# Layer 0's scales and shifts: modulation weights loaded into the array, conditioning vectors streamed

## The chip, the cores and the metric

The kernel runs on one core of one Trainium2 chip. The metric is device time in microseconds (us) of one execution: the median of several runs, lower is better. The engines of the core are TensorE (PE; its weight loads are shown apart as PEld), VectorE (DVE), ScalarE (ACT), GpSimd (POOL) and SyncE (SP, which issues nearly all DMAs here). They run their own instruction lists in program order and wait for each other by semaphores.

## What is computed

The reference is a two-layer diffusion backbone block over 1024 latent tokens and 256 context tokens, model width D = 1024, all in float32. Cut to what matters here, layer 0 begins with

```python
def adaln(cvec, w, b):                 # w: (1024, 3072)
    m = jax.nn.silu(cvec) @ w + b
    return jnp.split(m[..., None, :], 3, axis=-1)     # shift, scale, gate

def modulate(x, g, shift, scale):
    return rmsnorm(x, g) * (1.0 + scale) + shift

sh, sc, gt = adaln(c, ada_w_e[0], ada_b_e[0])         # for the latent tokens
h = modulate(x, norm_e[0], sh, sc)
shc, scc, gtc = adaln(c_ctx, ada_w_e[0], ada_b_e[0])  # for the context tokens
hc = modulate(ctx, norm_e[0], shc, scc)
# h and hc then go through h @ in_e (six column blocks), a pooling mixer, a gated conv mixer, out_e
```

The change concerns the shift and the scale: two vectors (silu(c) and silu(c_ctx), 1024 long) times a 1024 x 2048 matrix. Layer 1 and the gate of layer 0 get theirs elsewhere, on VectorE.

## The kernel before

Activations lie with the 1024 features on partitions (8 tiles of 128, index k) and the tokens along the free side, so shift and scale are wanted as columns: `mode[:, m, s]` holds feature 128*m+p on partition p for stream s (0 latent, 1 context).

The modulation matrix `ada_e` is read in 16 slabs of 128 x 1024 f32 (512 KB), `part` 1 (scale) first, then `part` 0 (shift), each k = 0..7. `ada(part, k)` (L452) takes one of three slots (`adp`, L433), issues the slab's DMA on SP's queue (L455), and issues two matmuls (L457): the loaded side is `cs[:, k, :]` (128 x 2: the two silu'd vectors), the streamed side is half of the slab (512 columns). The sums over k gather in four PSUM tiles `pr` of the pool `psd` as two rows of 512 columns. Each f32 matmul appears in the trace as two pairs of a weight load and a stream, so 32 matmuls are 64 pairs.

`ada_end(part)` (L459) turns the rows into columns. For each half q: the row is copied out of PSUM (L462, by the helper at L231 on ACT for q = 0, L233 on DVE for q = 1), four transposes on PE (L464) put 128 x 2 columns into `pm`, and DVE adds the bias into `mode` (L467). After part 1 two more DVE operations (L417) make `Ae` = norm * (1 + scale).

The order of the work is the program order of L504 to L532, the same on every queue:

- L504: slabs of part 1, and between them the loads of x's first 512 tokens (`fetch`, L447); the first projection weight is loaded (L294).
- L508: ACT squares x (L483) and DVE adds (L485); L509 `ada_end(1)`.
- L510: a ones matrix on PE (L312) sums the squares over partitions, then 1/rms on ACT and DVE (L375 to L387).
- L511: DVE scales x by `Ae` and 1/rms (L512). L513: slabs of part 0.
- L516 to L519: ACT casts projection weights to their high halves (`wh`, L267) and POOL makes the low halves (`wl`, L268); SP issues the loads of the next weight, of tokens 512 to 1023 and of the context.
- L520 `ada_end(0)`. L524: ACT adds the shift and rounds (`hi`, L526), DVE makes the remainder (`lo`, L527), k by k. In between the squares of the second token block run on ACT, POOL (L481) and DVE.
- From there the projections: `dense` (L302), for each k three fp32r products of 128 x 512 (`wl` by hi, `wh` by lo, `wh` by hi). After the first 36 of them PE is given the ones matmuls for the second token block and for the context (L312), then goes on.

The `dense` tiles of L302 come from the same PSUM pool as the four `pr` tiles.

Of the kernel before, what the change touches and what calls it, by code (L numbers as in the profile page):

```python
# [8 lines left out]
F32 = mybir.dt.float32  # L9
F32R = mybir.dt.float32r  # L10
AF = mybir.ActivationFunctionType
ALU = mybir.AluOpType
# [167 lines left out]
class Kern:  # L180
# [241 lines left out]
    def layer_even(self, es):  # L422
        tc, nc, A = self.tc, self.nc, self.A
        self.psd = es.enter_context(tc.tile_pool(name="psd", bufs=4, space=PSUM))
        psa = es.enter_context(tc.tile_pool(name="psa", bufs=2, space=PSUM))
        mode = self.cp.tile([128, 24, 2], F32, name="mode")
        cs = self.cp.tile([128, 8, 2], F32, name="cs")
        h = self.slots()
        ctx_norm = ExitStack()
        nrm = ctx_norm.enter_context(tc.tile_pool(name="nrm", bufs=2, side="right"))  # L430
        xin = ctx_norm.enter_context(tc.tile_pool(name="xin", bufs=2, side="right"))
        w0p = ctx_norm.enter_context(tc.tile_pool(name="w0p", bufs=1, side="right"))
        adp = ctx_norm.enter_context(tc.tile_pool(name="adp", bufs=3, side="right"))  # L433
        pm = psa.tile([128, 24, 2], F32, tag="pm", name="pm", bufs=1)
        nc.scalar.activation(out=cs[:, :, 0], in_=self.vcol("c", 0, 8), func=AF.Silu)
        nc.scalar.activation(out=cs[:, :, 1], in_=self.vcol("c_ctx", 0, 8), func=AF.Silu)

# [9 lines left out]
                nc.sync.dma_start(out=x, in_=(A["xT"] if src == "x" else A["ctxT"])[k, :, c0:c0 + n])  # L447
                xs.setdefault(b, []).append(x)

        pr = [self.psd.tile([128, 512], F32, tag="d", name="pr") for _ in range(4)]  # L450

        def ada(part, k):  # L452

            w = adp.tile([128, 1024], F32, tag="ad", name="ad")
            nc.sync.dma_start(out=w, in_=A["ada_e"][k, :, 1024 * part:1024 * part + 1024])  # L455
            for q in range(2):
                nc.tensor.matmul(pr[2 * part + q][0:2], lhsT=cs[:, k, :], rhs=w[:, 512 * q:512 * q + 512], start=(k == 0), stop=(k == 7))  # L457

        def ada_end(part):  # L459
            row = nrm.tile([2, 1024], F32, tag="row", name="row", bufs=1)  # L460
            for q in range(2):
                self.copy(("act", "dve")[q], row[:, 512 * q:512 * q + 512], pr[2 * part + q][0:2])  # L462
                for m in range(4 * q, 4 * q + 4):
                    nc.tensor.transpose(pm[:, 8 * part + m, :], row[:, 128 * m:128 * m + 128], self.cst("eye")[0:2, 0:2])  # L464
                o = slice(8 * part + 4 * q, 8 * part + 4 * q + 4)
                b = self.vcol("ada_b_e", 8 * part + 4 * q, 4).unsqueeze(2).to_broadcast([128, 4, 2])
                nc.vector.tensor_tensor(out=mode[:, o, :], in0=pm[:, o, :], in1=b, op=ALU.add)  # L467
            if part:
                self.Ae = self.mod_cols(mode, "norm_e", "Ae")

# [33 lines left out]
        for k in range(8):  # L504
            ada(1, k)
            fetch(XB[0], (k,))
        next(self.wit)
        *_, acc = squares(XB[0])  # L508
        ada_end(1)  # L509
        rs = rstd(XB[0], acc)  # L510
        for k, x in enumerate(X(XB[0])):  # L511
            nc.vector.scalar_tensor_tensor(out=x, in0=x, scalar=self.Ae[:, k, 0:1], in1=rs, op0=ALU.mult, op1=ALU.mult)  # L512
        for k in range(8):  # L513
            ada(0, k)
# [3 lines left out]
        next(self.wit)  # L518
        fetch(CB[0])  # L519
        ada_end(0)  # L520
        sq1 = squares(XB[1], (1, 3, 5))
        nc.vector.tensor_copy(mode[:, 16:24, 0], self.vcol("ada_b_e", 16, 8))
# [14 lines left out]
        def lines(t, off, pitch, src, c0, n, sh=0):  # L537

            if src == "x":
                p0 = off + pitch * (c0 // 64)  # L540
                a = t[:, p0 + sh:p0 + sh + 1]
                return bass.AP(tensor=a.tensor, offset=a.offset, ap=[list(a.ap[0]), [pitch, n // 64], [1, 64]])
            p0 = off + pitch * 16 + c0 + sh
            return t[:, p0:p0 + n]

        def flat(t, src, c0, n, as_lines=True):
            o = c0 + (0 if src == "x" else T)
            v = t[:, o:o + n]
            return v.rearrange("p (r t) -> p r t", t=64) if (src == "x" and as_lines) else v
# [18 lines left out]
        def first(b, side=True, order=(0, 1, 2)):  # L568

            ds = [self.dense(ws[i][0], rhs, (b,), ws[i][1]) for i in order]  # L570
            for _ in range(8 if side else 0):
                for d in ds[:2]:
                    for _ in range(3):
                        yield next(d)
            for d in ds:
                yield from d

        d = first(XB[0])
# [11 lines left out]
        d = first(XB[1])  # L590
# [5 lines left out]
        d = first(CB[0], False, (1, 0, 2))  # L596
# [55 lines left out]
        for i in range(4):  # L652
# [5 lines left out]
            bufs = [sa, sb]  # L658
            for lv in range(i + 1):
# [6 lines left out]
                m = 1 << lv  # L666
# [19 lines left out]
            w = next(self.wit)  # L686
            for _ in self.dense(w, rhs, BLK, lambda s, c0, n, ps: nc.vector.tensor_tensor(
                    out=lines(Q, 1, 65, s, c0, n), in0=ps.rearrange("p (r t) -> p r t", t=64) if s == "x" else ps,
                    in1=flat(gcs, s, c0, n), op=ALU.mult)):
                pass  # L690
            ada_on(2)
            for s, c0, n in (("x", 0, T), ("c", 0, TC)):
                o = flat(cv, s, c0, n)
                nc.vector.tensor_scalar(out=o, in0=lines(Q, 1, 65, s, c0, n), scalar1=self.vcol("sconv_w", 4 + i),
                                        scalar2=None, op0=ALU.mult)
                for tap, sh in ((0, -1), (2, 1)):
                    nc.vector.scalar_tensor_tensor(out=o, in0=lines(Q, 1, 65, s, c0, n, sh), scalar=self.vcol("sconv_w", 4 * tap + i),
                                                   in1=o, op0=ALU.mult, op1=ALU.add)
            w = next(self.wit)
            for _ in self.dense(w, rhs, BLK, lambda s, c0, n, ps: nc.vector.tensor_tensor(  # L700
                    out=flat(cv, s, c0, n, False), in0=ps, in1=flat(cv, s, c0, n, False), op=ALU.mult)):
                pass
            w = next(self.wit)
# [20 lines left out]
        for b in (BLK[0], BLK[2], BLK[1]):  # L724
# [3 lines left out]
            o = c0 + (0 if s == "x" else T)  # L728
# [70 lines left out]
        for m in range(4, 8):  # L799
# [6 lines left out]
            if m == 6:  # L806
                w = [next(self.wit)]
# [1591 lines left out]
```

## Time and profile before

| | us |
|---|---|
| median of 3 runs | 1560.08 |
| lowest, highest | 1555.54, 1568.76 |
| profiled execution, its own time | 1569.38 |
| its span (first to last instruction) | 1567.6 |
| mean granted TensorE clock in it | 0.938 of 2.4 GHz |

The rows below are from that one profiled execution. Times are from the start of the span. In a timeline a row is a run of like instructions, merged: start, length, engine, line, operation, tiles, shapes, count, and in brackets the engine's idle time just before and what ended it. The clock column gives the granted TensorE clock as a share of 2.4 GHz, 0.50 being 1.2 GHz; its records don't reach back to the first matmuls, where it shows 1.00 for want of one.

### The profile page before, as it was taken

Reading aid. Unit: us, or ns where it says so; the run is one execution under the profiler, and the core shown is the slowest. Engines: PE = TensorE matmul, PEld = TensorE weight load, DVE = VectorE, ACT = ScalarE, POOL = GpSimd, SP = SyncE. Lnnn points to the kernel's source line nnn. Section 1 sums busy time; section 2 is a strip of 40 time slices with the busy share of each in tenths; the row PEclk is TensorE's granted clock in tenths of the full one; section 3 lists DMA queues with packets and bytes.
Section 4 is the critical chain, followed back from the end, with each engine's and each line's share of the span. In section 5 each row is a group of like instructions: output and inputs, shape, how many; then the busy total and the mean of one; then the engine's idle time right before and its main releaser. Section 6 shows DMA issues by size and latency. Waiting matters only on the chain. (4 is left out here: it accounts for less than half of the span.)

```text
span 1567.6 us, 32131 instructions
## 1 busy us (share of the span) xinstructions
PE 1393.9 (89%) x12820; PEld 1092.7 (70%) x12820; DVE 1006.2 (64%) x1681; ACT 621.7 (40%) x1242; POOL 662.7 (42%) x925
## 2 busy tenths in 40 slices
PE   6899999999999998987988878898997988886996
PEld 1488888888888786865766656676775766674775
DVE  3746544347513732499999974878497677688567
ACT  2541111111423533445655521343454543557534
POOL 1352424252644532355565522755566246406004
PEclk9999999999999999999999989899998987878999
DMA  7413223222333112244544666655555566674233
GB/s 264 148 65 126 95 89 121 94 81 95 97 132 128 55 44 76 69 139 148 188 135 144 210 215 160 147 164 139 155 142 138 161 158 166 200 236 125 76 94 108
DMA packets 167894, 208.72 MB, mean 133 GB/s; under 512 B 38112, under 2 KB 129632, under 8 KB 167616
## 3 DMA queue, kind: packets, MB, share of 16 engines
q1 hardware_dynamic: 166448, 205.09, 43.4%
q8 instruction: 101, 1.65, 0.5%
q10 hardware_dynamic: 1296, 1.57, 0.3%
q14 instruction: 49, 0.40, 0.1%
HBM read 149.20 MB, written 55.44 MB: 131 GB/s over the span
## 5 line engine op out<-in xcount | busy, mean ns | idle before, releaser
L302 PE MATMUL d<-sx,wh 128*128 128x512 f32 x1152 | 361.6, 395 | 2.5 <-DVE sx L527 1.4
L302 PEld LDWEIGHTS d<-sx,wh 128*128 128x128 f32 x1152 | 217.2, 189 | 53.2 <-POOL sx L397 1.8
L302 PE MATMUL d<-sx,wl 128*128 128x512 f32 x576 | 229.8, 399 | 4.5 <-DVE u L822 2.7
L1396 POOL TENSOR_TENSOR tmp<-X,Bc 128x120 f32<-128x120 f32 (+2 forms) x300 | 122.1, 407 | 204.1 <-DMA Bc<-ED 181.9
L268 POOL TENSOR_TENSOR wl<-wr,wh 128x1024 fp32r<-128x1024 f32 x37 | 95.5, 2582 | 185.7 <-ACT wh L267 176.2
L992 PE MATMUL d<-sx,wh 128*128 128x512 f32 x512 | 167.5, 409 | 0.0
L1936 PE MATMUL d<-sx,wh 128*128 128x512 f32 x384 | 142.5, 439 | 0.0
L1397 POOL TENSOR_TENSOR X<-X,tmp 128x120 f32<-128x120 f32 (+2 forms) x300 | 120.1, 400 | 23.5
L302 PEld LDWEIGHTS d<-sx,wl 128*128 128x128 f32 x576 | 108.9, 189 | 29.7 <-issue 3.3
L628 DVE SCALAR_TENSOR_TENSOR junk<-wra,cb 128x1024 bf16<-128x1024 f32 x56 | 91.5, 1635 | 52.1 <-DMA wra<-in_ada_o 30.5
L992 PEld LDWEIGHTS d<-sx,wh 128*128 128x128 f32 x512 | 102.3, 200 | 23.9 <-issue 2.9
L992 PE MATMUL d<-sx,wl 128*128 128x512 f32 x256 | 116.2, 454 | 0.0
L302 PE MATMUL d<-sc,wh 128*128 128x256 f32 x576 | 104.1, 281 | 0.0
L1936 PE MATMUL d<-sx,wl 128*128 128x512 f32 x192 | 84.1, 438 | 7.4 <-DVE wl L1910 7.4
L1957 DVE SCALAR_TENSOR_TENSOR acc<-hc,vec,acc 128x960 f32<-128x960 f32 (+14 forms) x120 | 89.3, 769 | 1.1
L302 PEld LDWEIGHTS d<-sc,wh 128*128 128x128 f32 x576 | 88.8, 190 | 1.4
L1936 PEld LDWEIGHTS d<-sx,wh 128*128 128x128 f32 x384 | 75.6, 203 | 16.9 <-issue 0.2
L267 ACT CAST wh<-wr 128x1024 fp32r<-128x1024 f32 x37 | 38.7, 1045 | 117.3 <-PE d L302 86.8
L302 PE MATMUL d<-sc,wl 128*128 128x256 f32 x288 | 81.0, 281 | 0.0
L1498 PE MATMUL sc<-w,bk 64*128 64x128 f32 (+1 forms) x640 | 55.9, 313 | 21.7 <-DMA bk<-BKD 14.1
L1498 PEld LDWEIGHTS sc<-w,bk 64*128 64x128 f32 x640 | 47.0, 212 | 30.2 <-issue 24.9
L1512 DVE TENSOR_TENSOR w<-sc,cstb 64x256 f32<-64x256 f32 x80 | 33.8, 422 | 43.1 <-PE sc L1498 26.4
(380 smaller groups left out, 2909.8 us busy)
## 6 DMA issues: line engine op xcount, KB each, us to landing
wr<-in_in_o SPq DMA_DIRECT2D x32, 512.0 KB
wr<-in_in_e SPq DMA_DIRECT2D x24, 512.0 KB
wra<-in_ada_o SPq DMA_DIRECT2D x24, 512.0 KB
BKD<-bk SPq DMA_DIRECT2D x40, 256.0 KB
BTD<-X SPq DMA_DIRECT2D x20, 512.0 KB
bk<-BKD SPq DMA_DIRECT2D x40, 256.0 KB
Bc<-ED SPq DMA_DIRECT2D x20, 512.0 KB
bkt<-BTD SPq DMA_DIRECT2D x40, 256.0 KB
```

The lines of the kernel that those rows point to most:

```text
L267: self.nc.scalar.copy(hi, raw)
L268: self.nc.gpsimd.tensor_tensor(out=lo, in0=raw, in1=hi.bitcast(F32), op=ALU.subtract)
L302: self.nc.tensor.matmul(ps[:, :n], lhsT=w[a][:, k, :], rhs=rhs(src, k, b, c0, n), start=(i == 0), stop=(i == len(seq) - 1))
L628: nc.vector.scalar_tensor_tensor(out=junk, in0=w, scalar=1.0, in1=cb[:, s, :], op0=ALU.mult, op1=ALU.mult, accum_out=dst[:, s:s + 1])
L992: nc.tensor.matmul(ps, lhsT=w[a][:, k, :], rhs=rhs(s, k, b, c0, m), start=(q == 0), stop=(q == len(seq) - 1))
L1396: g.tensor_tensor(out=t, in0=X[:, :, j:j + 1].to_broadcast([128, 8, m]), in1=B[:, j, :, j + 1:16] if j < 8 else B2[:, j - 8, :, j - 7:8], ...
L1397: g.tensor_tensor(out=X[:, :, j + 1:16], in0=X[:, :, j + 1:16], in1=t, op=ALU.add)
L1498: nc.tensor.matmul(ps[h][:, d, i, h:h + 1] if ctx else ps[h][:, d, i], lhsT=bk[R[h], c, d, i], rhs=w[R[h], c, d, sl, i, :], start=True, st ...
L1512: nc.vector.tensor_tensor(out=w[o, c, :, 2 * h], in0=ps[h][o, :, :, h], in1=ma[o].unsqueeze(2).to_broadcast([64, 2, 2, 64]), op=ALU.mult)
L1936: nc.tensor.matmul(ps, lhsT=wt(a, k), rhs=rhs("x", k, b, c0, 512), start=(i == 0), stop=(i == len(seq) - 1))
L1957: nc.vector.scalar_tensor_tensor(out=acc[:, o], in0=hc[:, q], scalar=w, in1=acc[:, o], op0=ALU.mult, op1=ALU.add)
```

## The change

The two operands of the matmul in `ada` change places. A slab's 128 x 128 block m is now the loaded side and the 128 x 2 vectors are streamed past it, so the result is already a pair of columns. Per slab there are 8 matmuls in the place of 2; per part 64, the sums of all m and k of a part sharing one PSUM tile of 128 x 8 x 2. The `pr` tiles, the row copies and the transposes go. The bias is added once for a part instead of once for half of it. `pm` becomes two tiles, one for each part. Slabs, slots, DMAs and the order of L504 to L532 stay.

```diff
-        pm = psa.tile([128, 24, 2], F32, tag="pm", name="pm", bufs=1)
+        pm = [psa.tile([128, 8, 2], F32, tag=f"pm{i}", name="pm", bufs=1) for i in range(2)]
...
-        pr = [self.psd.tile([128, 512], F32, tag="d", name="pr") for _ in range(4)]
-
         def ada(part, k):
 
             w = adp.tile([128, 1024], F32, tag="ad", name="ad")
             nc.sync.dma_start(out=w, in_=A["ada_e"][k, :, 1024 * part:1024 * part + 1024])
-            for q in range(2):
-                nc.tensor.matmul(pr[2 * part + q][0:2], lhsT=cs[:, k, :], rhs=w[:, 512 * q:512 * q + 512], start=(k == 0), stop=(k == 7))
+            for m in range(8):
+                nc.tensor.matmul(pm[part][:, m, :], lhsT=w[:, 128 * m:128 * m + 128], rhs=cs[:, k, :], start=(k == 0 and m == 0), stop=(k == 7 and m == 7))
 
         def ada_end(part):
-            row = nrm.tile([2, 1024], F32, tag="row", name="row", bufs=1)
-            for q in range(2):
-                self.copy(("act", "dve")[q], row[:, 512 * q:512 * q + 512], pr[2 * part + q][0:2])
-                for m in range(4 * q, 4 * q + 4):
-                    nc.tensor.transpose(pm[:, 8 * part + m, :], row[:, 128 * m:128 * m + 128], self.cst("eye")[0:2, 0:2])
-                o = slice(8 * part + 4 * q, 8 * part + 4 * q + 4)
-                b = self.vcol("ada_b_e", 8 * part + 4 * q, 4).unsqueeze(2).to_broadcast([128, 4, 2])
-                nc.vector.tensor_tensor(out=mode[:, o, :], in0=pm[:, o, :], in1=b, op=ALU.add)
+            o = slice(8 * part, 8 * part + 8)
+            b = self.vcol("ada_b_e", 8 * part, 8).unsqueeze(2).to_broadcast([128, 8, 2])
+            nc.vector.tensor_tensor(out=mode[:, o, :], in0=pm[part], in1=b, op=ALU.add)
             if part:
                 self.Ae = self.mod_cols(mode, "norm_e", "Ae")
```

## Rows read from the trace of the kernel before

**Rows 1.** The page: its span, and its chain that ended last, by engine as shares of the span.
```profile
span 1567.6 us, 32131 instructions
...
PE 15%; DMA 9%; DVE 7%; POOL 4%; SPq 3%; issue 2%; ACT 2%; DVEq 0%; ACTq 0%; POOLq 0%
```

**Rows 2.** Ten windows of 50 us, from 70 to 570 us: busy time (instructions) of PE, PEld, DVE, ACT and POOL, clock, DMA share, GB/s. The first window, and the sum of the ten.
```profile
70.00:120.00 50.00, 48.48 (x255) 40.50 (x254) 24.45 (x36) 23.94 (x41) 19.79 (x13) 1.00 0.17 61
...
sum 500.00, PE 494.43 PEld 414.27 DVE 243.02 ACT 132.66 POOL 207.36; mean PE 49.44 PEld 41.43 DVE 24.30 ACT 13.27 POOL 20.74
```

**Rows 3.** The timeline, from the first slab to the start of part 0.
```profile
7.40 9.43 PE L457 MATMUL pr<-ad,cs 128*2 128x512 f32 x16 [7.40 <-DMA ad<-in_ada_e]
...
11.00 0.33 SPq L455 DMA_DIRECT2D ad<-in_ada_e  x1
...
25.39 1.88 PE L457 MATMUL pr<-ad,cs 128*2 128x512 f32 x4 [1.04 <-DMA ad<-in_ada_e]
...
26.98 0.69 DVE L485 TENSOR_TENSOR acc<-acc,sq 128x512 f32<-128x512 f32 x1 [2.44 <-ACT sq L483]
...
27.46 0.41 PE L464 MATMUL pm<-cstt,row 2*128 2x2 f32 x4 [0.19 <-ACT row L231]
...
27.99 0.67 DVE L233 COPY row<-pr 2x512 f32<-2x512 f32 x1
...
28.71 0.41 PE L464 MATMUL pm<-cstt,row 2*128 2x2 f32 x4 [0.84 <-DVE row L233]
...
29.05 1.13 PE L312 MATMUL a<-acc,cstt 128*128 128x512 f32 x2
...
30.10 7.08 PE L457 MATMUL pr<-ad,cs 128*2 128x512 f32 x16
...
34.72 7.35 DVE L512 SCALAR_TENSOR_TENSOR x<-x,Ae,rs 128x512 f32<-128x512 f32 x8
```

**Rows 4.** The timeline, from the last slabs of part 0 to the projections.
```profile
39.23 8.72 PE L457 MATMUL pr<-ad,cs 128*2 128x512 f32 x16 [2.04 <-DMA ad<-in_ada_e]
...
47.33 1.04 ACT L267 CAST wh<-wr 128x1024 fp32r<-128x1024 f32 x1 [13.16 <-DMA wr<-in_in_e]
48.28 0.57 ACT L231 COPY row<-pr 2x512 f32<-2x512 f32 x1
...
49.55 1.95 ACT L526 ACTIVATE sx<-x,mode 128x512 fp32r<-128x512 f32 x3 [0.70 <-DVE mode L467]
...
50.49 0.50 PE L302 MATMUL d<-sx,wl 128*128 128x512 f32 x1
...
50.82 7.82 DVE L527 SCALAR_TENSOR_TENSOR sx<-x,mode,sx 128x512 fp32r<-128x512 f32 x5
...
62.48 2.84 PE L312 MATMUL a<-acc,cstt 128*128 128x512 f32 x6
...
67.96 0.70 PE L312 MATMUL a<-acc,cstt 128*128 128x256 f32 x2 [2.63 <-DVE acc L485]
68.31 0.58 PE L302 MATMUL d<-sx,wl 128*128 128x512 f32 x1
```

**Rows 5.** The timeline of PE and PEld: rows from which the prices of a load and of a stream are read, at either level of the clock.
```profile
10.76 0.13 PEld L457 LDWEIGHTS pr<-ad,cs 128*2 128x2 f32 x1 [0.72 <-issue]
11.62 0.13 PEld L457 LDWEIGHTS pr<-ad,cs 128*2 128x2 f32 x1 [0.72 <-issue]
12.38 0.09 PEld L457 LDWEIGHTS pr<-ad,cs 128*2 128x2 f32 x1 [0.63 <-issue]
12.81 0.09 PEld L457 LDWEIGHTS pr<-ad,cs 128*2 128x2 f32 x1 [0.34 <-issue]
...
27.46 0.32 PEld L464 LDWEIGHTS pm<-cstt,row 2*128 2x128 f32 x4 [1.12 <-ACT row L231]
...
29.05 0.30 PEld L312 LDWEIGHTS a<-acc,cstt 128*128 128x128 f32 x2
...
53.61 0.33 PEld L302 LDWEIGHTS d<-sx,wl 128*128 128x128 f32 x1
...
54.04 0.63 PE L302 MATMUL d<-sx,wl 128*128 128x512 f32 x1
...
54.46 1.06 PE L302 MATMUL d<-sx,wh 128*128 128x512 f32 x2
...
68.72 0.63 PE L302 MATMUL d<-sx,wh 128*128 128x512 f32 x2
...
69.19 0.39 PE L302 MATMUL d<-sx,wl 128*128 128x512 f32 x1
...
96.07 0.19 PEld L302 LDWEIGHTS d<-sc,wl 128*128 128x128 f32 x1
96.19 0.31 PEld L302 LDWEIGHTS d<-sc,wh 128*128 128x128 f32 x2
```

**Rows 6.** Windows, with the columns of rows 2: two of 3 us early in the kernel, and two that follow each other late in it.
```profile
39.00:42.00 3.00, 2.77 (x4) 0.47 (x5) 3.00 (x5) 0.00 (x0) 0.00 (x0) 0.60 0.52 194
...
54.00:57.00 3.00, 3.00 (x9) 2.36 (x8) 3.00 (x3) 2.12 (x4) 2.84 (x3) 0.56 0.52 154
...
1449.50:1452.90 3.40, 1.67 (x129) 1.43 (x114) 3.23 (x7) 1.65 (x5) 0.00 (x0) 0.97 0.06 22
1452.90:1456.30 3.40, 3.40 (x33) 2.83 (x30) 2.58 (x6) 0.84 (x2) 0.00 (x0) 0.53 0.02 5
```

## The prediction

> **What bounds the kernel now.** I read the page first, then PE's windows, then the timeline of the first 70 us. The chain that ended last takes 42% of the 1567.6 us span, summed over its engines [rows 1], so it begins near 910 us and says nothing of the prelude that the change touches. What a us of the prelude is worth must come from the windows behind it: from 70 to 570 us PE is busy 494.4 of 500 us [rows 2]. PE runs its list in program order, nearly without a gap, from the restart of the projections at 68.3 us [rows 4]. A us by which that restart moves is a us at the end; later lists are in program order too, so I pass it on one to one.
>
> In the prelude the reader is to follow PE. Part 1 runs from 7.40 us; its last slab lands at 25.39 and PE is through at 27.27. Then copy, transposes, copy, transposes, and only at 29.05 the ones matmul; part 0 starts at 30.10 [rows 3]. Part 0 ends at 47.95 (39.23 + 8.72); ACT is in a weight cast until 48.37, copies a row, and the first shift is added at 49.55; the first product of the projections starts at 50.49 [rows 4].
>
> **The change, part by part.**
>
> *What goes.* Two row copies on ACT and two on DVE, 16 transposes on PE, two bias additions. On the path: behind part 1, the 1.78 us from 27.27 to 29.05 [rows 3], of which only what the ones matmul needs otherwise stays, the sum of squares at 27.67 (26.98 + 0.69). Behind part 0, 1.6 us from 47.95 to 49.55 [rows 4], of which some 0.25 us stay for the bias addition and its wait; while the cast runs until 48.37, that is the floor.
>
> *What comes.* Per slab 8 f32 matmuls of two pairs, so 16 pairs of a 128-column load and a two-column stream, where there were 4 pairs of a two-column load and a 512-column stream; 256 pairs for 64. No DMA, queue or slot moves: a slot is freed when its slab's last pair is done, as now (SP issues the fourth slab at 11.00, just behind the first four pairs) [rows 3].
>
> *Price of an old pair.* Loads at 10.76 and 11.62 start 0.86 us apart, at 12.38 and 12.81 0.43 us apart [rows 5]: PE was first at 1.2 GHz and rose to 2.4. A slab is 3.4 us at the lower level, 1.72 at the higher.
>
> *Price of a new pair.* The trace has no 128-column load before a two-column stream except the transposes, from two partitions: four loads in 0.32 us, about 0.06 to 0.08 each, the lower end. The ones matmul has two f32 loads of the full 128 x 128: together 0.30 us, the second alone 0.19 (as at 96.07), so they start 0.11 apart. Loads at 96.07 and 96.19, beside streams of 256 columns, start 0.12 apart [rows 5]. Upper end: one load ends before the next begins, 0.19. I take 0.107 to 0.12 at 2.4 GHz, the ones matmul being the same kind of load: a slab costs 1.7 to 1.9 us. At 1.2 GHz I double it, as the old pairs doubled: 0.213 each, 3.4 us a slab; ends 0.12 (twice the transposes') and 0.33, the length of one load at that level at 53.61 [rows 5]. So at the same clock the swap costs PE nothing. The question is the clock.
>
> *The clock.* It rose at 12.4 us while PE streamed 512-column blocks against loads of 0.13 us, so loading was not what raised it. It fell to 0.60 in 39 to 42, behind a wait of 2.04 us for a slab [rows 4, 6]. It fell to 0.53 at 1452.9, behind a stretch in which PE was busy 1.67 and PEld 1.43 of 3.40 us with 129 short matmuls: loads over 42% of the stretch did not hold it up [rows 6]. After the change PE has, in both parts, only loads and streams of two columns. No row shows just that, but those nearest say that loading does not carry the clock. I take 1.2 GHz for both parts.
>
> A rule of the Trainium skill stands against this. "TensorE: Matmul & The Clock Gate", section LDWEIGHTS, gives a load as its columns over 1.2 in ns, 107 ns for 128, and names no dependence on the clock. By it slabs would cost 1.7 us at any level and the sum would be that of the first rival. The rows differ: 0.33 us for one load at 53.61 against 0.19 at 96.07 [rows 5].
>
> *The sum at 1.2 GHz.* Part 1: 7.40 + 8 x 3.41 = 34.7. The slabs don't wait: the last lands at 25.39 with today's pace, and one slot is freed every 3.4 us; the squares, done at 27.67 now, come up to 5 us later, still in time. The ones matmul follows at once; at half clock its two streams take 2 x 0.85 = 1.7 us, so PE is free at 36.5, where it was at 30.10: +6.4. Part 0: 36.5 + 27.3 + 0.2 (drain) = 64.0, against 47.95: +16.1. x's scaling on DVE (now until 42.1 [rows 3]) moves with the ones matmul to about 49 and stays hidden, and so does the second weight's load and cast, whose DMA stands behind the last slab, issued 10 us ahead of the end. Then 0.25 us to the first shift: 64.25 against 49.55, **+14.7**. The removed copies and transposes are in this (1.78 us behind part 1, 1.35 behind part 0).
>
> *What is given back.* From the first product to the restart PE now takes 17.8 us: 36 products until 62.4, paced by DVE's `lo`, five in 7.82 us while POOL squares beside it; 2.84 us of ones matmuls; 2.63 us of waiting for the context's sum [rows 4]. In the new order the second token block lands before the shift is known, so POOL's squares are partly done by then. But the products start at 1.2 GHz: 0.42 us each (54.04 to 54.46) against 0.235 (0.47 for two, 68.72 to 69.19) [rows 5]; now that level holds from 54 until about 56.6 [rows 6]. With 5 us of it the 36 take some 11 us, about as long as now. So it is the 2.63 us wait that can shrink. Between none and all of it: +12.1 to +14.7; I take **+12.5**, since POOL's early start serves just that wait.
>
> So 1569.4 + 12.5 = 1581.9 for the profiled execution, which is 9.3 us above the median of the runs. For the median 1560.1 + 12.5 = 1572.6: 0.8% slower. About 1% (15.6 us) is what a measurement of this kernel can tell from no change.
>
> **Rivals.**
>
> *A. The loads run as at 2.4 GHz*, because the clock stays up after all or, by the page's rule, because they don't follow it. For it: PEld and PE would both be busy through the parts, and no row has just this mix. Against: rows 6, and 0.33 us at 53.61. Its price: part 1 stays bound by the last slab (25.39 + 1.85), the ones matmul waits only for the squares, 27.7 for 29.05, part 0 starts 1.35 us sooner and ends about 1.0 sooner, since slabs 12 to 15 wait for their DMAs as now. Without copies the shift comes at 47.4 for 49.55, behind the cast: -2.1, and DVE's first `lo` -2.7. Sum -2.4: 1557.7. It is a gain in every case in which a slab stays under 2 us.
>
> *B. Loads and streams follow one another*, at 1.2 GHz: a load has to end before the next starts. Then a pair is 0.33 us, a slab 5.3, both parts 84.5 instead of 54.6 us: 30 more, +42, 1602, 2.7% slower. It passes 1% from 0.225 us per pair on (256 x 0.012 = 3.1 us beyond the forecast). For it: nothing but the length of a load's record. Against: transposes overlap, 0.14 each at 0.06 to 0.08 apart, and so do the ones loads [rows 5].
>
> *C. As forecast, but the prelude's end doesn't recover, or the projections stay at 1.2 GHz longer* than today: +15 to +18, 1575 to 1578, the edge of 1%.
>
> **How the numbers follow.** Forecast 0.66, A 0.13, B 0.05, C 0.16. Forecast and C lie 11 to 18 us up; two medians of such runs scatter by some 4 us (1555.5 to 1568.8 in three runs). Own range of the likeliest: 1565 to 1580. A's 1557.7 is near enough to take in for two in ten; B is left out. Range 1557 to 1581. Slower by over 1%: B, three fifths of C and a tenth of the forecast, 0.05 + 0.09 + 0.07 = 0.21. Faster by over 1%: none of the cases reaches 1544.5, 0.02 for scatter. Within 1%: 0.77.
>
> **What would show it.** Right: loads of L457 with 128 columns, 256 of them, 0.21 us apart in both parts; granted clock 0.5 until the projections; ones matmul (L312) at 34 to 36 us; first L526 at about 64; restart after the second L312 at about 80; nothing new behind that. The step on the clock is wrong if loads start 0.11 apart and part 1 still ends at 27 (A); the price of a pair is wrong if they stand 0.3 apart (B); the return is wrong if L526 moves by 14.7 and the restart by the same (C). The forecast is wrong as a whole if the first L526 comes before 50 us.

## The result, and the profile after

Six runs of the changed kernel have a median of 1577.61 us (1575.1 to 1583.33), six of the kernel before in the same comparison 1558.96. The ratio of the two kernels, by which all kernels here are compared, is 1.0106 with a 95% interval of 1.0075 to 1.0137 (the quotient of the two medians is 1.0120, inside it): slower by about 1%. Forecast: 1572.6 us, range 1557 to 1581.

The page after (profiled execution 1575.1 us): its span, and its chain by engine.

```profile
span 1573.3 us, 32476 instructions
...
PE 50%; DVE 19%; DMA 9%; POOL 7%; issue 6%; ACT 6%; SPq 3%; DVEq 0%; POOLq 0%; ACTq 0%
```

The shares add up to 100%: this time the chain is followed back to the start of the span, where before it covered 42% [rows 1]. On it, 3% of the span is the two parts of this change; the page gives `PE pm L455` that share. (In the changed file `ada`'s DMA is L453, its matmul L455, the bias addition L460; x's scaling is L505, `hi` L519, `lo` L520.)

The timeline of after, from the first slab to the restart; it answers to [rows 3, 4].

```profile
7.48 27.38 PEld L455 LDWEIGHTS pm<-cs,ad 128*128 128x128 f32 x128 [7.48 <-issue]
7.51 27.44 PE L455 MATMUL pm<-cs,ad 128*128 128x2 f32 x128 [7.51 <-DMA ad<-in_ada_e]
...
11.08 0.33 SPq L453 DMA_DIRECT2D ad<-in_ada_e  x1
...
14.49 0.33 SPq L453 DMA_DIRECT2D ad<-in_ada_e  x1
...
30.31 0.69 DVE L478 TENSOR_TENSOR acc<-acc,sq 128x512 f32<-128x512 f32 x1 [2.61 <-ACT sq L476]
...
34.81 2.05 PE L312 MATMUL a<-acc,cstt 128*128 128x512 f32 x2
...
36.65 27.31 PE L455 MATMUL pm<-cs,ad 128*128 128x2 f32 x128
...
41.41 7.35 DVE L505 SCALAR_TENSOR_TENSOR x<-x,Ae,rs 128x512 f32<-128x512 f32 x8
...
59.87 1.04 ACT L267 CAST wh<-wr 128x1024 fp32r<-128x1024 f32 x1 [19.02 <-DMA wr<-in_in_e]
...
63.99 0.17 DVE L460 TENSOR_TENSOR mode<-pm,vec 128x16 f32<-128x16 f32 x1 [15.24 <-PE pm L455]
...
64.20 1.95 ACT L519 ACTIVATE sx<-x,mode 128x512 fp32r<-128x512 f32 x3 [3.29 <-DVE mode L460]
...
64.96 6.42 DVE L520 SCALAR_TENSOR_TENSOR sx<-x,mode,sx 128x512 fp32r<-128x512 f32 x5 [0.52 <-ACT sx L519]
...
65.07 0.76 PE L302 MATMUL d<-sx,wl 128*128 128x512 f32 x1 [1.11 <-ACT sx L519]
...
65.94 1.22 PE L302 MATMUL d<-sx,wh 128*128 128x512 f32 x2
...
75.60 2.74 PE L312 MATMUL a<-acc,cstt 128*128 128x512 f32 x6
...
80.70 0.70 PE L312 MATMUL a<-acc,cstt 128*128 128x256 f32 x2 [2.37 <-DVE acc L478]
...
81.05 0.58 PE L302 MATMUL d<-sx,wl 128*128 128x512 f32 x1
```

The first two rows hold the whole answer: 128 pairs in 27.44 us, 0.214 us a pair, merged into one row because PE never paused between slabs. The slab DMAs follow PE: issues at 11.08 and 14.49 are 3.41 us apart, one slab of pairs. Part 0 takes 27.31 us. The clock records of this execution begin only at 69.0 us, at 2.4 GHz. That PE stood at 1.2 GHz before is read from its rows: the ones matmul takes 2.05 us where it took 1.13 [rows 3]. Against before:

| us from the start | before | after | moved | forecast |
|---|---|---|---|---|
| PE free for part 0 | 30.10 | 36.65 | +6.6 | +6.4 |
| part 0 ends | 47.95 | 63.96 | +16.0 | +16.1 |
| first shift (`hi`) | 49.55 | 64.20 | +14.65 | +14.7 |
| restart of the projections | 68.31 | 81.05 | +12.74 | +12.5 |

Behind the restart the same delay is carried on. One POOL row (a low half, L268) in the trace of before, then in that of after:

```profile
377.20 3.06 POOL L268 TENSOR_TENSOR wl<-wr,wh 128x1024 fp32r<-128x1024 f32 x1 [11.05 <-ACT wh L267]
```

```profile
389.90 2.71 POOL L268 TENSOR_TENSOR wl<-wr,wh 128x1024 fp32r<-128x1024 f32 x1 [11.04 <-ACT wh L267]
```

It is 12.70 us late, and like instructions stay 12.6 to 12.9 us late up to 640 us. Windows of 50 us from 70 to 570 us show PE busy 492.1 of 500, 494.4 before [rows 2].

### The profile page after: what moved, and what is told of

Same layout as the page of the kernel before. It is cut to its first block, busy times and chain, and to the rows that moved or that the text cites. A ratio compares the mean times of both kernels' runs of the same rounds, so it can differ in the third digit from the quotient of the medians.

```text
span 1573.3 us, 32476 instructions
## 1 busy us (share of the span) xinstructions
PE 1410.2 (90%) x12996; PEld 1138.7 (72%) x12996; DVE 1005.9 (64%) x1677; ACT 621.6 (40%) x1240; POOL 660.2 (42%) x925
## 3 DMA queue, kind: packets, MB, share of 16 engines
q8 instruction: 102, 1.67, 0.5%
## 4 chain that ended last, share of the span: by engine, by line
PE 50%; DVE 19%; DMA 9%; POOL 7%; issue 6%; ACT 6%; SPq 3%; DVEq 0%; POOLq 0%; ACTq 0%
PE d L302 27%; DMA Bc<-ED 4%; PE d L985 4%; PE pm L455 3%; PE d L1929 3%; POOL X L1390 3%; PE d L2071 3%; POOL tmp L1389 3%; PE d L913 2%; DVE acc L1950 1%; DMA bk<-BKD 1%; PE sc L1491 1%; DVE ar L1217 1%; DVE thw L1166 1%; PE d L2276 1%
## 5 line engine op out<-in xcount | busy, mean ns | idle before, releaser
L1389 POOL TENSOR_TENSOR tmp<-X,Bc 128x120 f32<-128x120 f32 (+2 forms) x300 | 118.0, 394 | 202.1 <-DMA Bc<-ED 179.8
L268 POOL TENSOR_TENSOR wl<-wr,wh 128x1024 fp32r<-128x1024 f32 x37 | 95.8, 2588 | 200.3 <-ACT wh L267 200.3
```

The lines of the kernel that those rows point to most:

```text
L268: self.nc.gpsimd.tensor_tensor(out=lo, in0=raw, in1=hi.bitcast(F32), op=ALU.subtract)
L1389: g.tensor_tensor(out=t, in0=X[:, :, j:j + 1].to_broadcast([128, 8, m]), in1=B[:, j, :, j + 1:16] if j < 8 else B2[:, j - 8, :, j - 7:8], ...
```

## The experiments

The question after the result: are the 12.7 us the clock (two-column streams leave PE at 1.2 GHz), or is a pair with a 128-column load that dear at any clock? And does 12.7 us explain the medians?

**The changed kernel again**, as a reference on the chip of the next three runs. No edit.

> The changed kernel once more, to size its end-to-end cost against what its prelude shows. In its trace the restart of the projections stands 12.7 us later than before and the lag stays 12.7 until about 660 us. Theory 1 (the prelude's 12.7 us is all; the rest of the measured 18.6 us of the medians is scatter of single executions): the ratio to before comes out nearer 1.0082, 1.005 to 1.011. Theory 2 (something behind the prelude costs 6 us more in most executions): 1.011 to 1.014.

Measured: 1581.13 (6 runs) against 1565.5 (17 runs), ratio 1.0098 [1.0076, 1.0119]. First shift 64.27, restart 81.38, then 13.0 us late through 640 us. The late stages differ from execution to execution. The row `y<-y,y` of L2255 near the end in the first trace of the changed kernel, then in this one:

```profile
1533.64 1.29 POOL L2255 TENSOR_TENSOR y<-y,y 128x512 f32<-128x512 f32 x1 [85.20 <-ACT y L2248]
```

```profile
1540.12 1.29 POOL L2255 TENSOR_TENSOR y<-y,y 128x512 f32<-128x512 f32 x1 [86.12 <-ACT y L2248]
```

6.5 us between two executions of one kernel, where at 390 us they stood 0.35 apart. So no single execution says what the prelude costs at the end; only the ratios can. 12.7 us of 1560 is 1.0081, inside both intervals, and both centres (1.0106, 1.0098) lie above it.

**128 columns streamed.** The swap is kept, but the two vectors are repeated 64 times, so that each 128-column load is followed by a stream of 128 columns in place of two; the results go to four tiles of 512 columns.

```diff
+        csw = nrm.tile([128, 8, 128], F32, tag="csw", name="csw", bufs=1)
+        nc.vector.tensor_copy(csw.rearrange("p k (r s) -> p k r s", s=2), cs.unsqueeze(2).to_broadcast([128, 8, 64, 2]))
...
-                nc.tensor.matmul(pm[part][:, m, :], lhsT=w[:, 128 * m:128 * m + 128], rhs=cs[:, k, :], ...)
+                nc.tensor.matmul(pr[2 * part + m // 4][:, 128 * (m % 4):128 * (m % 4) + 128], lhsT=w[:, 128 * m:128 * m + 128], rhs=csw[:, k, :], ...)
```

> As the changed kernel, with 128 streamed columns in the place of two (the two vectors repeated 64 times; only the first two columns of each result are read, sums gather in the four former PSUM tiles). Same loads, same number of instructions, same DMAs; streams are longer, beside the loads. Theory 1 (a load costs 0.21 us because the clock stands at 1.2 GHz, and the clock stands there because next to nothing is streamed): loads start 0.21 us apart at first, then 0.107 to 0.12 from 12 to 13 us on; part 1 ends near 27.3 us for 34.9, part 0 near 47, the first shift (L526) at 47 to 48 for 64.2, the restart at 65 to 67 for 81; end-to-end 0.9985 of before (-2.4 us), 0.990 of the changed kernel. Rival (the load costs 0.21 us in this use whatever is streamed): part 1 at 35 us, restart at 81, ratio 1.008 to before. Second rival (long streams don't hide behind the loads): 0.21 us per pair even at 2.4 GHz, about the same times as the changed kernel, with the granted clock up.

Measured: 1567.33 (12 runs), ratio to before 1.0006 [0.9987, 1.0024]. The timeline of this kernel:

```profile
25.77 2.05 PE L458 MATMUL pr<-csw,ad 128*128 128x128 f32 x16 [0.67 <-DMA ad<-in_ada_e]
...
27.88 1.12 PE L312 MATMUL a<-acc,cstt 128*128 128x512 f32 x2
...
29.46 7.41 PE L458 MATMUL pr<-csw,ad 128*128 128x128 f32 x64 [0.46 <-DMA ad<-in_ada_e]
...
47.31 1.94 ACT L523 ACTIVATE sx<-x,mode 128x512 fp32r<-128x512 f32 x3
...
48.06 8.36 DVE L524 SCALAR_TENSOR_TENSOR sx<-x,mode,sx 128x512 fp32r<-128x512 f32 x5 [0.56 <-ACT sx L523]
...
50.44 0.73 PE L302 MATMUL d<-sx,wh 128*128 128x512 f32 x2 [1.80 <-DVE sx L524]
...
61.37 2.84 PE L312 MATMUL a<-acc,cstt 128*128 128x512 f32 x6 [0.96 <-DVE acc L482]
...
67.25 0.70 PE L312 MATMUL a<-acc,cstt 128*128 128x256 f32 x2 [3.04 <-DVE acc L482]
```

64 pairs in 7.41 us are 0.116 a pair, with 64 times the columns. Its clock records begin at 10.8 us, at 2.4 GHz, and just there the loads go from 0.213 to 0.112 us apart. PE waits for slabs again. The stream of 128 columns costs nothing beside its load; the first shift stands at 47.31, 2.2 us ahead of before. That is rival A's timeline (47.4), reached by another stream. A part of it is scatter: in the other executions with this prelude the first shift stands at 46.71 to 48.38, in those with the prelude of before at 48.00 to 49.63. But the restart came at 67.60, only 0.7 ahead; 65 to 67 was expected. 1.5 us went between shift and restart, in three waits of PE: 1.80 us for the first `lo` where it was 1.43, 0.96 for the second block's sum where none is shown, and 3.04 for the context's sum where it was 2.63 [rows 4]. On DVE five `lo` take 8.36 us, 7.82 before.

**Each part alone.** Part 0 in the new form with part 1 in the old, and the reverse; one execution each.

```diff
+            if part == 0:        # in the other kernel: part == 1
+                for m in range(8):
+                    nc.tensor.matmul(pn[:, m, :], lhsT=w[:, 128 * m:128 * m + 128], rhs=cs[:, k, :], ...)
+                return
             for q in range(2):
                 nc.tensor.matmul(pr[2 * part + q][0:2], lhsT=cs[:, k, :], rhs=w[:, 512 * q:512 * q + 512], ...)
```

> Only part 0 (shifts) in the new form; part 1 with its copies and transposes as before. Theory 1: part 1 ends at 27.3 and part 0 starts at 30.1 us as before, at first with loads 0.11 us apart, as the clock is up from part 1 and the ones matmul, then 0.21; part 0 ends at 53 to 57.5 for 47.95; first shift 5 to 8 us later than before, restart 3 to 7 later. Rival (load price independent of the clock): 0.21 from its first pair, part 0 ends at 57.5.

> Only part 1 (scales) in the new form. Theory 1: part 1 ends at 34.9, ones matmul until 36.9 at half clock; part 0 in the old form starts with pairs 0.86 apart and comes to 0.43 after some 3 to 6 us, as in part 1 of before; part 0 ends at 53.5 to 56, with its copy chain the first shift at 55 to 57.5, 5.5 to 8 us later than before. With the part-0-only kernel the two delays at the restart add up to 12.7 within 2 us.

Measured: part 0 alone 1571.41, first shift 57.32, restart 73.58 (+5.3); part 1 alone 1564.45, first shift 57.75 (expected 55 to 57.5), restart 76.73 (+8.4). 5.3 + 8.4 is 13.7 against 12.7, so the two parts nearly add up at the restart; one execution says nothing of the end. Part 0 alone is the case in which PE comes to the pairs at 2.4 GHz, and here the clock's records cover them. Its rows, and windows of 3 us (busy us and instructions of PE, PEld, DVE, ACT, POOL, then the clock, DMA share, GB/s):

```profile
29.25 0.19 PEld L459 LDWEIGHTS pn<-cs,ad 128*128 128x128 f32 x1 [0.24 <-issue]
...
29.77 27.30 PE L459 MATMUL pn<-cs,ad 128*128 128x2 f32 x128
```

```profile
27.00:30.00 3.00, 2.03 (x12) 1.35 (x13) 1.50 (x6) 1.36 (x2) 0.00 (x0) 0.93 0.93 373
30.00:33.00 3.00, 3.00 (x15) 3.00 (x16) 1.44 (x2) 2.00 (x4) 0.00 (x0) 0.50 0.04 18
...
45.00:48.00 3.00, 3.00 (x16) 3.00 (x16) 0.00 (x0) 0.00 (x0) 0.00 (x0) 0.50 0.46 158
```

The reader is to see 0.50 beside PE and PEld that are busy all 3 us. I had expected some slabs at 0.11 first; there were none. Part 0 ends at 57.07, where the rival had it (57.5), so this kernel alone doesn't tell a pair that is dear at any clock from a low clock. By the clock's records it fell at 29.6 us, 0.3 us after part 0's first load and before its first two-column stream; before that PE had waited for the row copies, with eight short transposes and the ones matmul between (busy 2.03 of the 3 us). So the pairs didn't bring the fall. What came with them is that it lasted, until 63.7 us. In two kernels further down whose part 0 streams 512 columns as before (the later restart, and the context's sum later on the kernel before) the records show a fall at the same place, at 29.3 and 30.3 us, and 2.4 GHz again from 32.7 and 33.7. Windows of the first of them:

```profile
30.00:33.00 3.00, 3.00 (x5) 0.47 (x5) 1.44 (x2) 1.88 (x3) 0.00 (x0) 0.54 0.04 15
33.00:36.00 3.00, 3.00 (x8) 0.60 (x7) 2.75 (x3) 1.09 (x2) 1.83 (x1) 1.00 0.48 175
```

**Unread streams between the slabs.** The changed kernel, and per slab two f32 matmuls of 512 columns whose result nobody reads (added work).

```diff
+            for q in range(2):
+                nc.tensor.matmul(dm[0:2], lhsT=cs[:, k, :], rhs=w[:, 512 * q:512 * q + 512], start=True, stop=True)
```

> The changed kernel with extra work: behind the 16 pairs of each slab PE also streams the slab's two halves against the vectors, as the kernel before did (4 more pairs of 512 columns a slab), into a PSUM tile that nobody reads. Theory 1 (two-column pairs cost 0.21 us only because the clock stands at 1.2 GHz): from the first rise of the clock on the loads stand 0.107 to 0.12 us apart, a slab costs 1.75 + 1.72 = 3.5 us with the extra work, as much as 3.4 without it; first shift (L526) within 3 us of the changed kernel's 64.2, where it falls back between slabs somewhat later. Rival (a 128-column load with a two-column stream costs 0.21 us at either clock): 3.41 + 1.72 = 5.1 us a slab, part 1 ends at 48, first shift at 91 to 93 us.

Measured (one execution): 1593.77, first shift 89.56, restart 106.37. The timeline of its PE:

```profile
7.69 3.55 PE L457 MATMUL pm<-cs,ad 128*128 128x2 f32 x16 [7.69 <-DMA ad<-in_ada_e]
11.17 3.57 PE L459 MATMUL dm<-ad,cs 128*2 128x512 f32 x4
...
49.71 3.58 PE L457 MATMUL pm<-cs,ad 128*128 128x2 f32 x16
53.21 3.57 PE L459 MATMUL dm<-ad,cs 128*2 128x512 f32 x4
56.71 2.26 PE L457 MATMUL pm<-cs,ad 128*128 128x2 f32 x16
58.90 1.88 PE L459 MATMUL dm<-ad,cs 128*2 128x512 f32 x4
...
65.26 1.95 PE L457 MATMUL pm<-cs,ad 128*128 128x2 f32 x16
67.13 1.88 PE L459 MATMUL dm<-ad,cs 128*2 128x512 f32 x4
```

I expected the clock to rise early and the first shift near 64; the clock's records begin at 57.4 us, at 2.4 GHz, and until there both kinds of row stand at the price of 1.2 GHz. So my picture of what raises it was too simple, and why it rose there stays open. The first shift is near the rival's 91 to 93 us, but not by the rival's way, a pair that is dear at either clock. For the trace shows the price of the new pair at both levels in one kernel: the same 16 pairs of a 128-column load and a two-column stream take 3.5 us before the rise and 1.9 after it (65.26 to 67.13), while the four unread streams go from 3.5 to 1.8. So the pair isn't dear by itself: its loads start 0.213 us apart at 1.2 GHz, and 0.112 at 2.4.

"TensorE: Matmul & The Clock Gate" of the Trainium skill, section LDWEIGHTS, gives a load as its columns over 1.2 in ns, 107 for 128, without the clock. The spacing of the loads at 2.4 GHz here (112 ns) is near it; at 1.2 GHz it is 213, and the measurement decides.

**Where the 1.5 us between shift and restart go.** Three kernels without the second token block's squares on POOL (ACT and DVE do them all): with 128 streamed columns, the kernel before, and with 128 streamed columns and four unread f32 matmuls ahead of the first slab, to have the clock up earlier.

```diff
-        sq1 = squares(XB[1], (1, 3, 5))
+        sq1 = squares(XB[1])
```

> The wide-stream kernel, with the squares of the second token block all on ACT and their sums all on DVE (before: three of eight squares and two additions on POOL). It asks where the 2.2 us went by which the wide-stream kernel's first shift came sooner (47.3 for 49.55) while its restart came only 0.7 sooner (67.6). Theory: DVE's lo operations run at 1.5 to 1.7 us beside POOL's squares and 0.74 alone, and both the sum that ACT waits for and the 36 products are paced by them. Then lo falls to under 0.9 us each, the second ones matmul comes at 58 to 60 us for 61.4, the restart at 63 to 65.5 for 67.6, end to end 0.9970 to 0.9985 of before. Rival (the restart is set by the arrival of the context's tiles or by the next weight's cast): the restart stays at 66.5 to 68.

> The kernel before with that same edit alone (squares of the second token block on ACT and DVE). Theory: first shift at 49.5 as before, restart 2.5 to 4 us sooner than 68.3, so 64.5 to 66; end to end 0.998. Rival: no change of the restart.

> The wide-stream kernel without POOL squares, and before the first slab lands (7.4 us) four f32 matmuls of 512 columns on a constant tile, result unread, so that the clock is up when the slab comes. Theory: the first slab costs 1.8 for 3.4 us, its slot is freed 1.6 us sooner, the DMA pause near 10 us shrinks, part 1 ends 0.5 to 1.5 us sooner, restart 0.5 to 1.5 us sooner than without; end to end 0.9965 to 0.998 of before. Rival (part 1 is bound by the DMAs alone, or the extra matmuls run into the first slab): no gain.

Measured: ratios 1.0012 [0.9985, 1.0038], 0.9994 [0.9975, 1.0013] and 1.0042 [1.0018, 1.0066]. DVE is freed as expected; in the first of the three:

```profile
50.85 2.73 DVE L524 SCALAR_TENSOR_TENSOR sx<-x,mode,sx 128x512 fp32r<-128x512 f32 x4
```

0.68 us each, where beside POOL's squares it was 8.36 / 5 = 1.67. Yet nothing came out at the end. In the kernel before without POOL's squares the restart came at 65.88, 2.4 us early and in the expected range (64.5 to 66). But 1.55 us of that stand there already at the first shift (48.00 for an expected 49.5), which the edit doesn't touch, so some 0.9 us are its own. And like instructions stand only 0.05 us early from 190 us on. Its windows around the restart show why:

```profile
60.00:63.00 3.00, 0.91 (x3) 0.08 (x1) 2.79 (x3) 1.03 (x3) 1.71 (x1) 1.00 0.10 14
63.00:66.00 3.00, 0.78 (x3) 0.69 (x3) 2.50 (x6) 2.46 (x5) 0.00 (x0) 0.70 0.43 164
66.00:69.00 3.00, 3.00 (x9) 2.33 (x8) 2.15 (x4) 1.50 (x3) 0.00 (x0) 0.50 0.00 0
69.00:72.00 3.00, 3.00 (x11) 2.35 (x10) 2.29 (x6) 2.10 (x3) 0.00 (x0) 0.66 0.00 0
```

The products are done earlier but the context's sum is not, so PE waits 4.31 us in place of 2.63. The clock falls to 0.50 in that wait, and the first projections run at 1.2 GHz until about 71 us: 9 and 11 matmuls in 3 us. What the earlier restart gained is spent there. With 128 streamed columns it is the same (wait 4.76 us, restart 67.43 for an expected 63 to 65.5; the rival had 66.5 to 68). The third missed outright: the unread matmuls ran into the first slab (first pair 9.64 for 7.3), restart 67.33; like instructions stand 1.3 us late through 550 us, and why its ratio is up by 0.4% stays open.

**A later restart and nothing else.** The kernel before, and 18 unread f32 matmuls on PE behind part 0.

```diff
+        for i in range(18):
+            nc.tensor.matmul(wps[0:2], lhsT=wm[:, 0:2], rhs=wm, start=True, stop=True)
```

> The kernel before, its matmuls as they were, with 18 f32 matmuls of 512 columns on a constant tile (result unread, 0.85 us each at 2.4 GHz) on PE between part 0 and the shift's transposes. It asks what a later restart is worth at the end, without the changed form. First shift at 63.5 to 64.5 us, restart at 80 to 82 (11.5 to 13.5 us later than before). Theory 1 (a us of the prelude is a us at the end): ratio to before 1.0060 to 1.0105, as for the changed kernel run again (1.0098). Theory 2 (the changed form costs something more behind the prelude): the ratio here is 1.008 or less and that of the changed kernel stays above it by 0.002 or more.

Measured: 1574.6 (12 runs) against 1566.03 (29), ratio 1.0054 [1.003, 1.0077]: 8.5 us, 4.7 to 12.1. The rows of the added streams and of the restart:

```profile
46.98 15.61 PE L519 MATMUL a<-wm 128*2 128x512 f32 x36
...
78.53 0.59 PE L302 MATMUL d<-sx,wl 128*128 128x512 f32 x1
```

The first shift came at 63.16 (expected 63.5 to 64.5). The restart moved by 10.2 (expected 11.5 to 13.5), and like instructions are 10.6 us late through 510 us. 10.6 us of 1566 is 1.0068, inside the interval, so one to one is consistent with it. By the words of the expectation, though, it is theory 2 that came out: 1.0054 is below theory 1's range, and the changed kernel's 1.0098 is 0.0044 above it. Of the 6.8 us between the two (15.3 and 8.5), 2.1 are the smaller delay, 10.6 us for 12.7; the other 4.7 are no more than the two intervals leave open.

**The context's sum later.** The context's ones matmul is moved behind 16 more products, so that PE need not wait for it; on the kernel with 128 streamed columns and on the one before.

```diff
-        apply_c = scaled_modulated(CB[0], rstd(CB[0], acc_c))
...
+        apply_c = scaled_modulated(CB[0], rstd(CB[0], acc_c))
```

> The wide-stream kernel with the context's ones matmul issued 16 products later on PE (after the 52nd product in the place of the 36th), so that PE doesn't stand waiting for the context's sum of squares. Theory: the restart in the wide-stream kernel (67.6 us) waits 3.0 us for that sum; with 16 products (3.8 us) in front the wait goes, PE is 2.5 to 3 us ahead at 120 us of the wide-stream kernel, 3 to 4 us ahead of the kernel before; end to end 0.9970 to 0.9985 of before. Rival (the second token block's high and low parts are then the bound, or the clock falls as in the kernel without POOL squares): less than 1 us ahead of the wide-stream kernel at 120 us.

> The kernel before with that same edit alone. Theory: 2 to 2.6 us ahead at 120 us (its wait is 2.63 us), end to end 0.9980 to 0.9995. Rival: nothing.

Measured: 1.0040 [1.0016, 1.0064] and 0.9986 [0.9962, 1.001]. The wait is gone from its place and turns up 10 us later, in the first kernel as

```profile
67.16 0.59 PE L312 MATMUL a<-acc,cstt 128*128 128x256 f32 x2
...
77.05 0.79 PE L302 MATMUL d<-sx,wl 128*128 128x512 f32 x1 [4.75 <-ACT sx L407]
```

where PE waits 4.75 us for ACT's `hi` of the second token block, and the windows of 3 us from 75 and 78 us show the clock at 0.50. The kernel before does the same (3.93 us at 78.44). Neither is ahead at 120 us as expected; in its one trace the first stands 0.3 us behind the kernel before through 550 us, the second 2.5 us. So the theory that the wait for the context's sum could be had for nothing fell. The two also show how loosely the end follows a small lag: the first one's ratio is worth +6.3 us (2.5 to 10.0), the second one's -2.2 us (-6.0 to +1.6). What moves the late stages by some us is shown by no run here.

## Why the prediction was right, and where it was not

- *The price of a pair follows the clock* (0.107 to 0.12 and 0.213): right, measured 0.112 and 0.214, and shown at both levels in the kernel with unread streams. The swap by itself is nearly free: 16 x 0.112 = 1.8 us a slab against 1.72.
- *PE stands at 1.2 GHz in both parts*: right, in part by luck. Both falls that it was taken from [rows 6] stand behind a stretch in which PE was idle for 2 us or half of the time, so those rows could not part loading from idling; after the change PE is never idle in the two parts. What settles it came later: widening the stream alone brought 2.4 GHz and took the whole loss away (1.0006 for 1.0098). What raises the clock is not known from this: in the kernel with unread streams it stayed down for 50 us beside streams of 512 columns. Rival A's condition, the loads at the price of 2.4 GHz, is what the kernel with 128 streamed columns shows; rival B fell with 0.214.
- *The sum through part 0 and the first shift*: right to 0.1 or 0.2 us at every step, the removed copies included: the ones matmul follows part 1 at once, and the first shift comes 0.24 us behind part 0.
- *What is given back*: the total was right (1.9 us of 0 to 2.6; I took 2.2), the place wrong, so that it fits is luck. The step that failed is "it is the 2.63 us wait that can shrink" and "the 36 take some 11 us, about as long as now". The wait shrank from 2.63 to 2.37 only. From first product to the second block's ones matmul it was 62.48 - 50.49 = 11.99 us and became 75.60 - 65.07 = 10.53: 1.46 of the 1.91 us. Nor are the 36 products paced by `lo`, as the prediction has it. PE waits for `lo` once, for the first of them; in the trace of before that is this row:

```profile
52.41 0.73 PE L302 MATMUL d<-sx,wh 128*128 128x512 f32 x2 [1.43 <-DVE sx L527]
```

After, the row at 65.94 shows no such wait. From the first product to this row it is 1.92 us before and 0.87 after, so 1.05 of the 1.46 us lie here; behind it PE's products follow one another at the clock's pace in both traces. That the first `lo` came sooner fits POOL's squares, which begin 1.7 us ahead of it now (63.30 and 64.96) and together with it before (50.76 and 50.82); without POOL's squares the kernel before waits 0.64 us there.
- *One to one to the end*: not contradicted, and not settled to better than some us. The trace gives +12.7 at the restart and at 640 us. By the ratios the end moved by 0.0106 x 1559 = +16.5 [11.7, 21.4] and 0.0098 x 1565.5 = +15.3 [11.9, 18.6]; the pure delay gave +8.5 [4.7, 12.1] for 10.6. The measured 1577.6 lies where rival C put it (1575 to 1578), but C's condition, a prelude's end that doesn't recover, did not come: 1.9 us were given back. Whether the changed form costs another 2 to 4 us in the late stages stays open; no run here tells it apart from scatter.

## What to carry to other kernels

Swapping the operands of thin f32 products moves the columns from the stream to the load and costs PE under 0.1 us a slab at one clock (1.8 for 1.72 us), but it can decide which clock PE gets; look for a row in which PE did just that mix, and if there is none, bound it at both levels. Here streams 64 times as wide were free and avoided the loss. And a few us won ahead of a PE wait can be lost behind it: follow the lag of like instructions a hundred us further before counting it, and don't take a lag of 2 us in one trace for a gain at the end.

## What the runs showed that I had not expected

- PE and PEld both busy all of a 3 us window at a granted clock of 0.50 (part 0 alone, 30 to 57 us).
- With a slab's two-column pairs and then its 512-column streams by turns the clock stayed at 1.2 GHz from 7.7 until 57.4 us, and then at 2.4 with the same mix.
- A 128-column f32 stream hides wholly beside a 128-column load: 0.116 us a pair at 2.4 GHz, where a slab of two-column pairs with unread streams behind it took 0.117 (1.87 us for 16).
- Three kernels show the clock falling behind the same row copies near 30 us; with 512-column streams behind them it was up again by 32.7 and 33.7 us, with two-column pairs not until 63.7.
- `lo` on DVE (128 x 512, two inputs) takes 0.68 us each with POOL's squares away, and 1.56 to 1.67 with them beside it.
